# q and k projections of all units ahead of attention, as 2x2 block products with seven products for eight

## The chip, the cores and the metric

The kernel runs on one core of a Trainium2 chip. The metric is the device time of one execution in microseconds (us). Engines are called PE (TensorE, matmuls and transposes), DVE (VectorE), ACT (ScalarE), POOL (GpSimd) and SP (SyncE, which issues most DMAs). Each engine runs its own instructions in their order; semaphores make one wait for another.

## What is computed

One layer of a transformer block on x of 1024 x 1024 in float32. The part that the change touches:

```python
h = rms_norm(x, g_pre_mix[l])
proj = h @ w_in[l]
sb_q, sb_k, sb_v = jnp.split(proj[..., :c0], 3, axis=-1)      # 8 heads of 64
d_q, d_k, d_v = jnp.split(proj[..., c0:c1], 3, axis=-1)        # 4 heads of 2 x 64
gates = jax.nn.sigmoid(proj[..., c1:])                          # 2 x 1024 columns
y_sb = stick_breaking_attention(sb_q, sb_k, sb_v)               # sigmoids and a running product
y_diff = differential_attention(q1, q2, k1, k2, d_v, lam, bias) # two softmaxes, one subtracted
merged = gate_sb * (y_sb @ w_sb_out[l]) + gate_diff * (y_diff @ w_diff_out[l])
x = x + rms_norm(merged @ w_o[l], g_post_mix[l])
```

An MLP with a squared ReLU follows (1024 to 4096 and back).

## The kernel before

Float32 accuracy comes from splitting: each operand is kept as a rounded part "hi" and a rest "lo", and a product is three matmuls, hi by hi, hi by lo, lo by hi. `load_split` (L95) loads a block of weights of 128 x 1024 (0.5 MB) on SP, casts it on ACT (L102) and subtracts on DVE (L103). h stands transposed in SBUF as h_hi and h_lo for the whole attention stage; `normalised` (L155) and `transpose_h` (L174) make it in two halves c of 512 rows.

Attention has eight units of work: four stick-breaking ones with two heads each (`steps_sb`, `finish_sb`), then four differential ones with one head, which is two maps (`steps_diff`, `finish_diff`). Per head or map there are eight query tiles of 128 rows, taken in pairs j in the order 3, 1, 2, 0. A pair's step issues its scores z (L262, L263), sigmoids on ACT (L322, L323), a mask on POOL (L326), a scan and a product on DVE (L331, L332); a step later its finish transposes the weights on PE (L281), splits them (ACT L287, DVE L288) and multiplies by v (L300, L301). In differential units DVE adds the bias and takes the minimum (L389), ACT takes the exponential, DVE combines both maps (L403, L404).

The queries and keys of a unit are made inside the unit before it. `prepare(u + 1)` (L463) yields pieces of `project_q`, `project_k` (16 blocks in all, each 2 x 24 matmuls of 512 columns in `project`, L189) and, every second unit, `project_v` for two units (8 tiles of 24 matmuls of 256 columns). Their accumulators acc_sbq, acc_sbk, acc_sbv, acc_dfq, ... are split into half tiles by ACT and DVE (L210, L211, L225, L226), and k is copied to the other half of the partitions by four DMAs (L230, L231). The gates (16 blocks like those of q, with their results kept in DRAM) are filler too: eight go into attention by the table GATES (L35), eight follow it (L530). The loop at L511 mixes a step, the finish of the step before, and pieces of filler by the steps' weights. A scheduler then sets the final order of the instructions on each engine, from dependences, buffers and the order written.

Pools limit what can be early: two accumulators "acc" for filler, two each of "sc", "av" and "tr" in PSUM; four tiles each of qs, kh and kl, three of v (each unit has one), four of w for split weights, two of raw.

Behind attention come the product with w_mix (L567), w_o (L656), the up projection, which takes 2x2 blocks with seven products already (L778 and the sums at L732 to L735 on POOL), and the down projection (L954).

## Time and profile before

| | |
|---|---|
| median of 3 runs | 1458.88 us (1458.36 to 1459.6) |
| span of the profiled execution | 1456.6 us |
| first scores to first product with w_mix | about 34 to 648 us |
| DMA, mean over the span | 151 GB/s |
| granted clock of PE, mean | 0.999 |

The profile holds one execution; its own time is its span and about 2 us around it, by the runs. "Busy" is the time in which an engine had an instruction in hand. The page cuts the span into 40 slices of 36 us and gives each engine's busy share in tenths (9 is 90% or more), and what the DMAs moved:

```profile
PE   7999999999999999999999999999999999999997
DVE  5477988898779876635556499767665669754783
POOL 2022322231000000000002335333330357232611
GB/s 206 73 138 64 72 48 81 65 73 48 83 85 66 75 122 180 162 196 139 162 120 244 238 151 195 187 151 142 143 161 205 252 286 178 209 243 273 197 287 58
```

PE is busy in all slices but the first and the last. DVE's share is highest in slices 4 to 10, the stick-breaking units.

### The profile page before, as it was taken

The numbers are of one execution on the slowest core, as the hardware profiler recorded it, in microseconds if no ns is written. First come the engines' busy times: TensorE is split into PE (matmuls) and PEld (weight loads), VectorE is DVE, ScalarE is ACT, GpSimd is POOL, SyncE is SP. The second block draws the span as 40 slices with busy tenths as digits, with TensorE's granted clock in tenths as the row PEclk, the third lists the DMA queues.
The fourth block names the chain that finished last, engine by engine and source line by source line (L and its number), as shares of the span: only waits on it lengthen the run. The fifth ranks groups of instructions, "written<-read, shape, count | busy, mean of one in ns | idle before, by whom it ended". The sixth has DMA issues, their size and how long they took to land.

```text
span 1456.6 us, 20071 instructions
## 1 busy us (share of the span) xinstructions
PE 1435.0 (99%) x7302; PEld 1220.3 (84%) x7302; DVE 1016.5 (70%) x1468; ACT 742.3 (51%) x1352; POOL 321.2 (22%) x312
## 2 busy tenths in 40 slices
PE   7999999999999999999999999999999999999997
PEld 6888898899889888888888878888888888888886
DVE  5477988898779876635556499767665669754783
ACT  6355765676556554763335364444444443534350
POOL 2022322231000000000002335333330357232611
PEclk9999999999999999999999999999999999999999
DMA  5241212221322245553437745544446785677681
GB/s 206 73 138 64 72 48 81 65 73 48 83 85 66 75 122 180 162 196 139 162 120 244 238 151 195 187 151 142 143 161 205 252 286 178 209 243 273 197 287 58
DMA packets 93946, 220.50 MB, mean 151 GB/s; under 512 B 9260, under 2 KB 24856, under 8 KB 93848
## 3 DMA queue, kind: packets, MB, share of 16 engines
q1 hardware_dynamic: 79448, 199.30, 42.8%
q10 hardware_dynamic: 14400, 19.93, 3.8%
q8 instruction: 57, 0.93, 0.3%
q14 instruction: 41, 0.34, 0.1%
HBM read 153.11 MB, written 60.05 MB: 146 GB/s over the span
## 4 chain that ended last, share of the span: by engine, by line
PE 94%; DVE 2%; DMA 1%; issue 1%; ACT 1%; POOL 0%; SPq 0%; POOLq 0%; DVEq 0%; ACTq 0%
PE dS L954 12%; PE dA L954 9%; PE mix L567 6%; PE o L656 6%; PE p_tr L778 5%; PE p_av L778 5%; PE c L778 4%; PE acc_gate L198 4%; PE acc_gate L196 4%; PE acc_gate L197 4%; PE p_sc L778 3%; PE z L263 2%; PE z L262 2%; PE tr_sb L281 2%; PE p L778 1%
## 5 line engine op out<-in xcount | busy, mean ns | idle before, releaser
L331 DVE TENSOR_TENSOR_SCAN rest<-rest 128x896 f32<-128x896 f32 (+3 forms) x64 | 87.6, 1374 | 20.6 <-POOL rest L326 20.3
L198 PE MATMUL acc_gate<-h_hi,lo_gate 128*128 128x512 f32 x256 | 101.0, 394 | 0.0
L196 PE MATMUL acc_gate<-h_hi,hi_gate 128*128 128x512 f32 x256 | 100.8, 394 | 0.0
L197 PE MATMUL acc_gate<-h_lo,hi_gate 128*128 128x512 f32 x256 | 100.7, 394 | 0.0
L608 DVE TENSOR_TENSOR lS_lo<-raw_S,lS_hi 128x1024 fp32r<-128x1024 f32 x32 | 56.2, 1757 | 39.8 <-ACT lS_hi L607 39.8
L326 POOL TENSOR_SCALAR_AFFINE_SELECT rest<-rest 128x128 f32<-128x128 f32 x64 | 23.5, 367 | 240.7 <-ACT rest L322 232.1
L954 PE MATMUL dS<-rT_hi,lS_hi 128*128 128x512 f32 x192 | 74.7, 389 | 0.0
L954 PE MATMUL dS<-rT_lo,lS_hi 128*128 128x512 f32 x192 | 74.7, 389 | 0.0
L954 PE MATMUL dS<-rT_hi,lS_lo 128*128 128x512 f32 x192 | 74.7, 389 | 0.0
L607 ACT CAST lS_hi<-raw_S 128x1024 fp32r<-128x1024 f32 x32 | 33.7, 1052 | 74.1 <-DMA raw_S<-s_dramS 33.8
L567 PE MATMUL mix<-y,hi_mix 128*128 128x512 f32 x256 | 68.6, 389 | 0.0
L394 ACT ACTIVATE s<-s,low 128x896 f32<-128x896 f32 (+7 forms) x64 | 49.7, 777 | 29.9 <-DVE low L389 29.7
L389 DVE CUSTOM_DVE_ANT_0 s<-z,bias 128x512 f32<-128x512 f32 (+3 forms) x64 | 37.0, 587 | 32.4 <-PE z L263 26.4
L567 PEld LDWEIGHTS mix<-y,hi_mix 128*128 128x128 f32 x256 | 48.0, 188 | 10.0
L198 PEld LDWEIGHTS acc_gate<-h_hi,lo_gate 128*128 128x128 f32 x256 | 48.2, 188 | 9.2
L197 PEld LDWEIGHTS acc_gate<-h_lo,hi_gate 128*128 128x128 f32 x256 | 48.2, 188 | 8.8
L196 PEld LDWEIGHTS acc_gate<-h_hi,hi_gate 128*128 128x128 f32 x256 | 48.2, 188 | 8.6
L116 POOL TENSOR_SCALAR rstd_o<-s 128x1 f32<-128x1 f32 x8 | 2.8, 356 | 236.5 <-DVE wa_lo L608 212.2
L287 ACT CAST wth_sb<-tr_sb 128x512 fp32r<-128x512 f32 (+1 forms) x80 | 41.2, 548 | 26.6 <-PE tr_sb L281 25.2
L326 POOL TENSOR_SCALAR_AFFINE_SELECT beta<-beta 128x128 f32<-128x128 f32 x64 | 53.9, 842 | 3.4 <-ACT beta L323 2.4
L288 DVE TENSOR_TENSOR wtl_sb<-tr_sb,wth_sb 128x512 fp32r<-128x512 f32 (+1 forms) x80 | 48.5, 627 | 7.7 <-ACT wth_sb L287 7.5
L778 PE MATMUL c<-hB_hi,wa_hi 128*128 128x512 f32 x128 | 50.0, 392 | 2.1 <-ACT p L798 2.1
(351 smaller groups left out, 4751.2 us busy)
## 6 DMA issues: line engine op xcount, KB each, us to landing
s_dramS<-us SPq DMA_DIRECT2D x64, 256.0 KB, 3.9
raw_S<-s_dramS SPq DMA_DIRECT2D x32, 512.0 KB, 4.4
s_dramA<-u ACTq DMA_DIRECT2D x48, 256.0 KB, 3.5
raw_A<-s_dramA SPq DMA_DIRECT2D x24, 512.0 KB, 3.8
raw_gate<-in_w_in_dram SPq DMA_DIRECT2D x16, 512.0 KB, 3.7
gate_dram<-gt SPq DMA_DIRECT2D x32, 256.0 KB, 2.5
y<-y_dram SPq DMA_DIRECT2D x16, 512.0 KB, 6.4
g<-gate_dram SPq DMA_DIRECT2D x16, 512.0 KB, 4.3
```

What stands on the lines that cost most here:

```text
L196: nc.tensor.matmul(acc, w_hi[:, ks], h_hi[k][:, cs], start=(k == 0), stop=False)
L197: nc.tensor.matmul(acc, w_hi[:, ks], h_lo[k][:, cs], start=False, stop=False)
L198: nc.tensor.matmul(acc, w_lo[:, ks], h_hi[k][:, cs], start=False, stop=(k == NK - 1))
L288: nc.vector.tensor_tensor(lo[:, :n], tr[:, :n], f32(hi[:, :n]), op=ALU.subtract)
L326: nc.gpsimd.affine_select(tl[:, dg], tl[:, dg], pattern=[[-1, P]], compare_op=ALU.is_gt, fill=fill, base=0, channel_multiplier=1,)
L331: nc.vector.tensor_tensor_scan(back, back, back, 1.0, op0=ALU.mult, op1=ALU.bypass)
L394: e = nc.scalar.activation(s[:, :nk], s[:, :nk], AF.Exp, bias=low, scale=-1.0, accum_out=sums[:, m:m + 1],)
L567: nc.tensor.matmul(accs[i][c], st[:, ks], mv[:, cs], start=(first and k % 4 == 0), stop=(last and k % 4 == 3),)
L608: nc.vector.tensor_tensor(lo, raw, f32(hi), op=ALU.subtract)
L656: nc.tensor.matmul(accs[n], st, mv[:, n * HALF:(n + 1) * HALF], start=(first and k == 0), stop=(last and k == NK - 1),)
L778: nc.tensor.matmul(acc, st[:, ks], mv, start=(first and k == 0 and i == 0), stop=(k == 3 and i == 2), skip_group_check=True,)
L954: nc.tensor.matmul(acc, st[:, e, ts], mv[:, e, :], start=(first and e == 0 and i == 0), stop=(last and e == 1 and i == 2))
```

## The change

A stage of its own now makes all q and k, with buffers of its own (23 "leaf" tiles of 0.5 MB, 8 "half" tiles of 0.25 MB). The two weight blocks of a unit (q and k) are the rows of a 2x2 block matrix, each cut into two halves of 512 along the model dimension; h is cut into four blocks, by model half and by row half. A Strassen-like scheme (in Winograd's form) needs seven block products of 12 matmuls (128 x 512, over 4 blocks of 128, three each) where the plain one has eight.

`first_two` computes the two products with h blocks 11 and 21, whose sum is q of the first rows; product one is also kept in DRAM. The sums T1 to T4 of h blocks are made once, on DVE and POOL, and split. `pair_sums` makes four sums of weights on POOL for each unit, `last_five` splits them, issues five products into the banks sc, av and tr, and adds them on DVE. `put` splits each quarter of the result and stores it to qk_dram on ACT's queue. The second row half of h is split again at the end (`split_late`), one part of it after a trip through DRAM.

In attention `load_qk(u + 1)` loads the ready parts at the start of unit u by 12 DMAs of 0.25 MB on SP. Filler is v (in odd units) and gates alone; 14 gates are now in attention, 2 behind it. The steps and finishes, the filler's loads and its evictions are issued with high priority for the scheduler.

```diff
-GATES = [range(0, 2), range(2, 2), range(2, 4), range(4, 4), range(4, 6), range(6, 6), range(6, 8), range(8, 8)]
+GATES = [range(0, 3), range(3, 4), range(4, 7), range(7, 8), range(8, 10), range(10, 11), range(11, 13), range(13, 14)]
...
+        def product_h(acc, w, name, first=True, last=True):
+            w_hi, w_lo = w
+            for k in range(4):
+                ks = slice(k * P, (k + 1) * P)
+                b_hi, b_lo = right_block(name, k)
+                for i, (st, mv) in enumerate(((w_hi, b_hi), (w_hi, b_lo), (w_lo, b_hi))):
+                    nc.tensor.matmul(
+                        acc, st[:, ks], mv, start=(first and k == 0 and i == 0), stop=(k == 3 and i == 2),
+                        skip_group_check=True,
...
+        def put(n, which, c, src):
+
+            stage = leaf(f"qk_{n}_{which}_{c}")
+            hi, lo = stage[:, 0, :], stage[:, 1, :]
+            if which == 0:
+                scale = SCALE if n < N_SB else -SCALE
+                nc.scalar.activation(hi, src, AF.Copy, scale=scale)
+                nc.vector.scalar_tensor_tensor(lo, src, scale, f32(hi), op0=ALU.mult, op1=ALU.subtract)
+            else:
+                nc.scalar.copy(hi, src)
+                nc.vector.tensor_tensor(lo, src, f32(hi), op=ALU.subtract)
+            nc.scalar.dma_start(out=qk_dram[n][:, which, :, c * HALF:(c + 1) * HALF], in_=f32(stage))
...
+        def first_two(n0, ws):
+
+            accs = [acc_tile(f"p12_{n0 + e}") for e in range(2)]
+            for e in range(2):
+                product_h(accs[e], halves(ws[e], 0), "B11")
+                p1 = half(f"p1_{n0 + e}")
+                nc.scalar.copy(p1, accs[e])
+                nc.sync.dma_start(out=p1_dram[n0 + e], in_=p1)
+            for e in range(2):
+                product_h(accs[e], halves(ws[e], 1), "B21", first=False)
+                put(n0 + e, 0, 0, accs[e])
...
+            for f, blk in zip((f0, f1), blks):
+                nc.sync.dma_start(out=f, in_=w_in[blk])
+            s1 = half(f"s1_{n}")
+            a11, a12, a21, a22 = (f[:, i * HALF:(i + 1) * HALF] for f in (f0, f1) for i in range(2))
+            nc.gpsimd.tensor_tensor(s1, a21, a22, op=ALU.add)
+            nc.gpsimd.tensor_tensor(a21, a11, a21, op=ALU.subtract)
+            nc.gpsimd.tensor_tensor(a11, s1, a11, op=ALU.subtract)
+            nc.gpsimd.tensor_tensor(a12, a12, a11, op=ALU.subtract)
+            return n, {"T1": s1, "T2": a11, "B22": a12, "T3": a21, "T4": a22}
...
+        def split_one(n, raw):
+            ring[0] += 1
+            if ring[0] % 2:
+                w = stream.tile([P, 2, HALF], F32R, tag="w", name=f"ws_{ring[0]}", bufs=4)
+            else:
+                w = big_pair(f"wl_{ring[0]}")
+            hi, lo = w[:, 0, :], w[:, 1, :]
+            nc.scalar.copy(hi, raw)
+            nc.vector.tensor_tensor(lo, raw, f32(hi), op=ALU.subtract)
+            return hi, lo
...
+        def last_five(n, ws):
+            b, d, c = (ps.tile([P, HALF], F32, tag=t, name=f"p_{t}{n}", bufs=2) for t in ("sc", "av", "tr"))
+            v, q, u21 = half(f"v_{n}"), half(f"q_{n}"), half(f"u21_{n}")
+            nc.sync.dma_start(out=v, in_=p1_dram[n])
+            w = {name: split_one(n, ws[name]) for name in ("T2", "T3", "T1", "T4", "B22")}
+            product_h(b, w["T2"], "T2")
+            nc.vector.tensor_tensor(v, b, v, op=ALU.add)
+            product_h(d, w["T3"], "T3")
+            nc.vector.tensor_tensor(q, d, v, op=ALU.add)
+            product_h(c, w["T1"], "T1")
+            nc.vector.tensor_tensor(q, c, q, op=ALU.add)
+            put(n, 1, 1, q)
+            product_h(d, w["T4"], "T4", first=False)
+            nc.vector.tensor_tensor(u21, d, v, op=ALU.add)
+            put(n, 1, 0, u21)
+            product_h(c, w["B22"], "B22", first=False)
+            nc.vector.tensor_tensor(v, c, v, op=ALU.add)
+            put(n, 0, 1, v)
...
+        first_two(0, ws)
+        normalise(1, xs1)
+        transpose_h(1, xs1)
+        for j in range(2):
+            whole_again(j)
+        first_two(2, [load_split(w_in[blocks_of(n)[0]], f"wa{n}") for n in (2, 3)])
+        r11, r21, r12, r22 = (raws[j, c] for j, c in ((0, 0), (1, 0), (0, 1), (1, 1)))
+        for q in range(2):
+            nc.sync.dma_start(out=r12_dram[q], in_=r12[q])
+        sums_h["T2"] = [leaf(f"t2_{q}", None, F32) for q in range(2)]
+        sums_h["T1"], sums_h["T3"], sums_h["T4"] = r11, r12, r21
+        for q in range(2):
+            nc.vector.tensor_tensor(r11[q], r12[q], r11[q], op=ALU.subtract)
+            nc.vector.tensor_tensor(sums_h["T2"][q], r22[q], r11[q], op=ALU.subtract)
+        for q in range(2):
+            nc.gpsimd.tensor_tensor(r12[q], r22[q], r12[q], op=ALU.subtract)
+        for q in range(2):
+            nc.gpsimd.tensor_tensor(r21[q], r21[q], sums_h["T2"][q], op=ALU.subtract)
+        first_two(4, [load_split(w_in[blocks_of(n)[0]], f"wa{n}") for n in (4, 5)])
+        split_sum("T2")
+        split_sum("T3")
+        first_two(6, [load_split(w_in[blocks_of(n)[0]], f"wa{n}") for n in (6, 7)])
+        summed = pair_sums(0)
+        split_sum("T1")
+        split_sum("T4")
+        split_late(1, r22)
+        for n in range(n_units):
+            ready = summed[1]
+            if n + 1 < n_units:
+                summed = pair_sums(n + 1)
+            last_five(n, ready)
+        r12 = [leaf(f"r12_again{q}", None, F32) for q in range(2)]
+        for q in range(2):
+            nc.sync.dma_start(out=r12[q], in_=r12_dram[q])
+        split_late(0, r12)
...
+        def load_qk(u):
+
+            qs, kh, kl = ([pa.tile([P, S], F32R, tag=n, name=f"{n}_{u}_{a}", bufs=4) for a in range(2)] for n in ("qs", "kh", "kl"))
+            for a, own in enumerate((LO, HI)):
+                for part in (LO, HI):
+                    nc.sync.dma_start(out=f32(qs[a][part]), in_=qk_dram[u][own, 0, 0 if part is LO else 1, :])
+                    nc.sync.dma_start(out=f32(kh[a][part]), in_=qk_dram[u][own, 1, 0, :])
+                    nc.sync.dma_start(out=f32(kl[a][part]), in_=qk_dram[u][own, 1, 1, :])
+            return qs, kh, kl
...
         def fill(u, gates):
-            if u + 1 < n_units:
-                yield from prepare(u + 1)
+            if u + 1 < n_units and u % 2:
+                yield from values(u + 1)
             for b in gates:
                 yield from gate(b)
...
+            if u + 1 < n_units:
+                operands[u + 1] = load_qk(u + 1)
+            size = 2 * len(GATES[u]) + (4 if u % 2 and u + 1 < n_units else 0)
             total = 36 * (2 if u < N_SB else 1)
-            for weight, finish in (steps_sb(u, *operands[u]) if u < N_SB else steps_diff(u - N_SB, *operands[u])):
-                if waiting is not None:
-                    waiting()
+            steps = steps_sb(u, *operands[u], vs[u]) if u < N_SB else steps_diff(u - N_SB, *operands[u], vs[u])
+            while True:
+                with tc.high_priority(offset=1500):
+                    weight, finish = next(steps, (0, None))
+                    if finish is not None and waiting is not None:
+                        waiting()
+                if finish is None:
+                    break
```

How instructions move, at three places. First PE at the end of unit 0 (names: tr_sb, z, av with unit, head, then pair or query tile; acc_sbq2 is filler for unit 2). In the kernel before, the first scores of unit 1 stand among filler:

```order
L262 MATMUL z_1_0_6_0_1576<-kh_sbk1_0_955,qs_sbq1_0_804 128x512
L263 MATMUL z_1_0_6_0_1576<-kl_sbk1_0_957,qs_sbq1_0_804 128x512
L262 MATMUL z_1_0_6_512_1581<-kh_sbk1_0_955,qs_sbq1_0_804 128x384
L263 MATMUL z_1_0_6_512_1581<-kl_sbk1_0_957,qs_sbq1_0_804 128x384
L198 MATMUL acc_sbq2_1_1667<-h_hi3_158,lo_sbq2_1635 128x512
L196 MATMUL acc_sbq2_1_1667<-h_hi4_159,hi_sbq2_1634 128x512
L197 MATMUL acc_sbq2_1_1667<-h_lo4_167,hi_sbq2_1634 128x512
L198 MATMUL acc_sbq2_1_1667<-h_hi4_159,lo_sbq2_1635 128x512
L196 MATMUL acc_sbq2_1_1667<-h_hi5_160,hi_sbq2_1634 128x512
L197 MATMUL acc_sbq2_1_1667<-h_lo5_168,hi_sbq2_1634 128x512
L198 MATMUL acc_sbq2_1_1667<-h_hi5_160,lo_sbq2_1635 128x512
L196 MATMUL acc_sbq2_1_1667<-h_hi6_161,hi_sbq2_1634 128x512
```

In the changed kernel the same attention work stands closely together:

```order
L460 MATMUL tr_sb0_1_2_1_2611<-ident_69,beta_0_1_4_2474 128x128
L460 MATMUL tr_sb0_1_2_1_2611<-ident_69,beta_0_1_5_2492 128x128
L460 MATMUL tr_sb0_1_2_1_2611<-ident_69,beta_0_1_4_2474 128x128
L460 MATMUL tr_sb0_1_2_1_2611<-ident_69,beta_0_1_5_2492 128x128
L441 MATMUL z_1_0_7_0_2681<-kh_1_0_1897,qs_1_0_1895 128x512
L442 MATMUL z_1_0_7_0_2681<-kl_1_0_1899,qs_1_0_1895 128x512
L479 MATMUL av_0_1_2_2597<-wth_sb0_1_2_0_2603,v_v0_0_1634 128x256
L441 MATMUL z_1_0_7_512_2686<-kh_1_0_1897,qs_1_0_1895 128x512
L442 MATMUL z_1_0_7_512_2686<-kl_1_0_1899,qs_1_0_1895 128x512
L480 MATMUL av_0_1_2_2597<-wtl_sb0_1_2_0_2604,v_v0_0_1634 128x256
L479 MATMUL av_0_1_2_2597<-wth_sb0_1_2_0_2603,v_v0_0_1634 128x256
L480 MATMUL av_0_1_2_2597<-wtl_sb0_1_2_0_2604,v_v0_0_1634 128x256
```

The filler of this place is gone: what PE had between a split on DVE and the matmul that reads it is now other attention work. The next filler rows are acc_v1_2, 37 rows further on.

Second, DVE at the same place. Before, with evictions of q and k (L211, L226) and a split of weights (L103) between the scans (L331, printed as SCALAR_TENSOR_TENSOR) and the products (L332):

```order
L103 TENSOR_TENSOR lo_sbv2_0_2053<-raw_sbv2_0_2050,hi_sbv2_0_2052 128x1024
L211 SCALAR_TENSOR_TENSOR qs_sbq2_0_1630<-acc_sbq2_1_1667,qs_sbq2_0_1630 64x512
L288 TENSOR_TENSOR wtl_sb0_1_2_2_1560<-tr_sb0_1_2_2_1555,wth_sb0_1_2_2_1559 128x384
L211 SCALAR_TENSOR_TENSOR qs_sbq2_1_1631<-acc_sbq2_1_1667,qs_sbq2_1_1631 64x512
L331 SCALAR_TENSOR_TENSOR rest_1_0_7_1593<-rest_1_0_7_1593 128x1024
L288 TENSOR_TENSOR wtl_sb0_1_0_0_1616<-tr_sb0_1_0_0_1611,wth_sb0_1_0_0_1615 128x384
L332 TENSOR_TENSOR beta_1_0_7_1592<-beta_1_0_7_1592,rest_1_0_7_1593 128x1023
L226 TENSOR_TENSOR kl_sbk2_0_1783<-acc_sbk2_0_1791,kh_sbk2_0_1781 64x512
L304 TENSOR_TENSOR part_0_1_2_1567<-av_0_1_2_1528,part_0_1_2_1567 64x256
L331 SCALAR_TENSOR_TENSOR rest_1_0_2_1697<-rest_1_0_2_1697 128x384
```

In the changed kernel (L510 is the scan, L511 the product, L467 the split of transposes, L483 and L486 the finish):

```order
L467 TENSOR_TENSOR wtl_sb0_1_2_1_2617<-tr_sb0_1_2_1_2611,wth_sb0_1_2_1_2616 128x512
L511 TENSOR_TENSOR beta_1_0_6_2661<-beta_1_0_6_2661,rest_1_0_6_2662 128x895
L510 SCALAR_TENSOR_TENSOR rest_1_0_7_2680<-rest_1_0_7_2680 128x1024
L467 TENSOR_TENSOR wtl_sb0_1_2_2_2629<-tr_sb0_1_2_2_2624,wth_sb0_1_2_2_2628 128x384
L486 TENSOR_TENSOR yt_0_1_1_2539<-part_0_1_1_2536,yt_0_1_1_2539 64x256
L467 TENSOR_TENSOR wtl_sb0_1_0_0_2703<-tr_sb0_1_0_0_2698,wth_sb0_1_0_0_2702 128x384
L511 TENSOR_TENSOR beta_1_0_7_2679<-beta_1_0_7_2679,rest_1_0_7_2680 128x1023
L510 SCALAR_TENSOR_TENSOR rest_1_0_2_2848<-rest_1_0_2_2848 128x384
L510 SCALAR_TENSOR_TENSOR rest_1_0_3_2861<-rest_1_0_3_2861 128x512
L483 TENSOR_TENSOR part_0_1_2_2636<-av_0_1_2_2597,part_0_1_2_2636 64x256
```

The evictions of q and k are gone from here, and attention's own instructions follow each other.

Third, SP where the new stage goes from first_two to last_five (raw_wa is the first weight block of a unit for first_two, fw the two blocks of a unit for pair_sums, v the re-read of product one). All of it is new:

```order
L98 DMA raw_wa6_624<-in_w_in_dram 128x1024
L98 DMA raw_wa7_630<-in_w_in_dram 128x1024
L280 DMA p1_dram4_164<-p1_4_558 128x512
L293 DMA fw0_0_700<-in_w_in_dram 128x1024
L280 DMA p1_dram5_165<-p1_5_573 128x512
L280 DMA p1_dram6_166<-p1_6_650 128x512
L293 DMA fw0_1_701<-in_w_in_dram 128x1024
L318 DMA v_0_745<-p1_dram0_160 128x512
L280 DMA p1_dram7_167<-p1_7_665 128x512
L293 DMA fw2_0_841<-in_w_in_dram 128x1024
```

fw0_1 stands behind raw_wa7, whose buffer it takes once that is split, and behind p1_dram6, a store of a product.

219 lines of the change are left out of this document (117 added, 102 removed).

## The prediction

> **What bounds the kernel now.** I read the page's busy times first, then the chain that ended last, then what TensorE (PE) waits for, then the table of stages.
>
> ```profile
> span 1456.6 us, 20071 instructions
> PE 1435.0 (99%) x7302; PEld 1220.3 (84%) x7302; DVE 1016.5 (70%) x1468; ACT 742.3 (51%) x1352; POOL 321.2 (22%) x312
> PE 94%; DVE 2%; DMA 1%; issue 1%; ACT 1%; POOL 0%; SPq 0%; POOLq 0%; DVEq 0%; ACTq 0%
> ...
> PE trx L178 <- DVE x L170: 7.7, 2, 7.5
> PE c L778 <- ACT p L798: 2.1, 1, 2.1
> PE p_sc L778 <- ACT w_hi L607: 1.2, 1, 1.2
> ```
>
> PE is busy 1435.0 of 1456.6 us. The rest is 21.6 us, 7.7 of it the wait for the first rows of x and only 3.3 in the two waits behind attention. So a matmul taken away is worth its full price only while nothing new waits, and work that PE does beside another engine's work is cover. The stages show how thick that cover is (each row: the stretch, its length, then busy us of PE, weight loads, DVE, ACT, POOL; clock, DMA share, GB/s):
>
> ```profile
> 0.00:33.00 33.00, 24.01 (x133) 20.06 (x134) 17.89 (x24) 21.12 (x34) 8.09 (x24) 1.00 0.65 228
> 172.00:294.00 122.00, 122.00 (x759) 109.37 (x758) 102.97 (x153) 77.43 (x181) 31.33 (x53) 1.00 0.23 66
> 368.00:654.00 286.00, 286.00 (x1591) 248.88 (x1590) 198.09 (x510) 167.38 (x352) 0.43 (x3) 1.00 0.39 122
> 860.00:1145.00 285.00, 284.40 (x1252) 234.96 (x1253) 205.66 (x224) 142.59 (x213) 84.16 (x56) 1.00 0.52 172
> ```
>
> In stick-breaking attention (172 to 294 is the second unit and what surrounds it) PE has no gap, but VectorE (DVE) is busy 103 of 122 us, 84%. The change takes PE work out of just this stage. The last row is the up projection, which already runs a seven-product scheme: PE 284.4 of 285. That speaks for the new projection stage.
>
> **What goes.** Prices of matmuls are start to start, since a duration of 0.39 us holds latency that overlaps. The first and last of 32 rows with 512 columns, and of 17 with 256:
>
> ```profile
> 1145.01 0.39 PE L954 MATMUL dA<-rB_lo,lA_hi 128*128 128x512 f32 x1
> 1152.04 0.39 PE L954 MATMUL dA<-rB_hi,lA_lo 128*128 128x512 f32 x1
> ...
> 23.72 0.28 PE L244 MATMUL acc_sbv<-kl_sbv,h_hi 128*128 128x256 f32 x1
> 25.64 0.28 PE L245 MATMUL acc_sbv<-qs_sbv,h_lo 128*128 128x256 f32 x1
> 40.01 1.91 PE L178 MATMUL trx<-ident,x 128*128 128x128 f32 x16
> ```
>
> 7.03 / 31 = 0.227 us for 512 columns, 1.92 / 16 = 0.12 for 256, 1.91 / 16 = 0.12 for a transpose. q and k took 16 blocks x 48 = 768 matmuls; the change takes 8 units x 7 products x 12 = 672. 96 x 0.227 = **-21.8 us**, the whole gain.
>
> **What attention has left.** Its DVE work, in groups over the four stick-breaking units, then the four differential ones (a count, then busy us and mean ns):
>
> ```profile
> L331 DVE TENSOR_TENSOR_SCAN rest<-rest 128x896 f32<-128x896 f32 (+3 forms) x64 | 87.6, 1374 | 20.6 <-POOL rest L326 20.3
> L288 DVE TENSOR_TENSOR wtl_sb<-tr_sb,wth_sb 128x512 fp32r<-128x512 f32 (+1 forms) x80 | 48.5, 627 | 7.7 <-ACT wth_sb L287 7.5
> L332 DVE TENSOR_TENSOR beta<-beta,rest 128x895 f32<-128x895 f32 (+3 forms) x64 | 47.9, 753 | 2.0
> L307 DVE TENSOR_TENSOR yt<-part,yt 64x256 fp32r<-64x256 f32 x32 | 13.2, 414 | 0.5 <-ACT yt L306 0.5
> ...
> L389 DVE CUSTOM_DVE_ANT_0 s<-z,bias 128x512 f32<-128x512 f32 (+3 forms) x64 | 37.0, 587 | 32.4 <-PE z L263 26.4 <-DMA bias<-bias_rows 5.7
> L404 DVE SCALAR_TENSOR_TENSOR s<-s,sums,s 128x896 f32<-128x896 f32 (+7 forms) x32 | 26.0, 812 | 0.4
> L288 DVE TENSOR_TENSOR wtl_df<-tr_df,wth_df 128x512 fp32r<-128x512 f32 (+1 forms) x40 | 24.4, 629 | 7.2 <-ACT wth_df L287 7.2
> L389 DVE CUSTOM_DVE_ANT_0 s<-z,bias,low 128x384 f32<-128x384 f32 (+3 forms) x32 | 17.5, 546 | 5.9 <-PE z L263 4.8
> L403 DVE TENSOR_SCALAR s<-s,sums 128x896 f32<-128x896 f32 (+7 forms) x32 | 16.6, 517 | 0.7
> L364 DVE SCALAR_TENSOR_TENSOR y<-y,subln,w 128x256 f32<-128x256 f32 x16 | 7.7, 480 | 0.3
> ...
> L103 DVE TENSOR_TENSOR lo_gate<-raw_gate,hi_gate 128x1024 fp32r<-128x1024 f32 x16 | 19.5, 1221 | 8.8 <-ACT hi_gate L102 6.8 <-PE avd L344 2.0
> L255 DVE TENSOR_TENSOR v_sbv<-acc_sbv,v_sbv 128x128 fp32r<-128x128 f32 x32 | 8.8, 281 | 8.2 <-ACT v_sbv L254 8.1
> L211 DVE SCALAR_TENSOR_TENSOR qs_sbq<-acc_sbq,qs_sbq 64x512 fp32r<-64x512 f32 x16 | 11.0, 689 | 7.7 <-ACT qs_sbq L210 7.3
> ```
>
> Stick-breaking units: 87.6 + 48.5 + 47.9 + 2 x 13.2 (L304 is as long as L307) = 210 us. v costs 16 x 0.28 + 2 x 1.22 = 6.9, a gate 1.22, q and k of one unit 8 x 0.69 + 2 x 1.22 = 7.9. On PE a head's 4608 score columns run twice (4.1 us), with 36 transposes (4.3), 32 value matmuls of 256 columns (3.8) and 8 of 128 (0.5): 25.4 us a unit, 101 in all; a v is 192 x 0.12 = 23.0, a gate 48 x 0.227 = 10.9, q and k of a unit 21.8. Before, these units carry four pairs of q and k, two v and four gates: PE 101 + 87 + 46 + 44 = 278, DVE 210 + 32 + 14 + 5 = 261, or 94%, and PE never waited. After, two v and eight gates: PE 101 + 46 + 87 = **234**, DVE 210 + 14 + 10 = **234**. The cover of 17 us is gone.
>
> Differential units: 37.0 + 17.5 + 26.0 + 24.4 + 16.6 = 121.5, and seven ops like L364 in each of 16 finishes, here 6.7 to 7.7 us a group, some 48; with read-outs of low and small ops about 188 us. After, one v and eight gates (two behind the last unit): DVE 188 + 7 + 10 = 205; PE 4 x 20.5 (as above with four short matmuls more per finish) + 23 + 87 = 192. Rows overlap a little at their ends (172 to 294 is 84% where the sums make 94%, part of it other work), so DVE is between 180 and 205 there.
>
> Where both engines need the same time, PE's idle time is set by how filler is spread. The order shows two places that I can price. At the end of unit 0 PE has 88 matmuls and transposes in a row, worth 11.2 us, of which only seven are filler: the v tiles have three buffers, so the evictions of the first two v1 products wait for unit 0's v, and both accumulators are held. In that stretch DVE has 23 instructions: two scans of 896 and 1024 (2.02 + 2.29), two mults (1.09 + 1.22), four shorter scans, seven splits of transposes, and small ones, 15.5 us with its two v splits. PE idles 15.5 - 11.2 = 4.3 us. v2 in unit 3 meets the same limit at the end of unit 2: about 5. In the differential units fill is drawn forward: between the first scores of units 5 and 6 PE has about 37 us of work and DVE 47 to 51, so 10 to 14 us, of which the transfer of the surplus before it gives back some; I take 11. Together **+20 us**; bounds 5 (DVE's slack of 6% as before is enough, only the two ends of units count half) and 40 (12.8 of DVE surplus, 9 at the two places, and every other unit's start and end at 3).
>
> **The projection stage.** Its PE work is 0.227 x 672 = 153 us. Prices from like rows of the up projection:
>
> ```profile
> L732 POOL TENSOR_TENSOR s<-raw_up 128x512 f32<-128x512 f32 x8 | 13.3, 1662 | 98.3 <-DMA raw_up<-in_w_up_dram 91.6 <-DVE w_lo L608 6.7
> L607 ACT CAST w<-s 128x512 fp32r<-128x512 f32 x16 | 9.9, 621 | 28.7 <-PE p_av L778 27.5 <-DVE hT_lo L608 0.7 <-POOL up L733 0.5
> L608 DVE TENSOR_TENSOR w<-s,w 128x512 fp32r<-128x512 f32 x16 | 21.7, 1359 | 0.1
> L865 DVE TENSOR_TENSOR v<-p_sc,p 128x512 f32<-128x512 f32 x12 | 8.2, 684 | 0.3 <-PE p_sc L778 0.3
> raw_gate<-in_w_in_dram SPq DMA_DIRECT2D x16, 512.0 KB, 3.7
> L608 DVE TENSOR_TENSOR rT_lo<-t,rT_hi 128x1024 fp32r<-128x1024 f32 x16 | 36.0, 2250 | 8.5 <-ACT rT_hi L607 8.5
> L608 DVE TENSOR_TENSOR rT_lo<-b_d,rT_hi 128x1024 fp32r<-128x1024 f32 x8 | 9.7, 1218 | 0.2 <-ACT rT_hi L607 0.2
> ```
>
> A unit's last five products are 60 x 0.227 = 13.6 us of PE. Beside them DVE has 5 PSUM adds and 3 put splits at 0.68 and 5 operand splits at 0.68 to 1.36: 8.8 to 12.3; ScalarE (ACT) 8 x 0.62 = 5; GpSimd (POOL) 4 x 1.66 = 6.6; SP two loads and one read. All hide: 0, up to 5 if the joints don't. The switch into this part hardly hides: fw0_1 stands on SP behind the store of p12_6's first product, when PE has some 45 products left (10.2 us); then 3.7 of load, three POOL ops (s1_1 lies between) of 1.66, one cast 0.62 and a split of 0.68 to 1.36 come to 10.0 to 10.7 us, and each of six hand-overs costs something more: +2 (0 to 5). At the start pair 0/1 has only 48 matmuls on the first half of x, where now the v products fill in; x_7 is the tenth load of 0.5 MB, 5.2 MB at 228 GB/s = 23 us, then its square, scale and turn: +3 (1 to 4). Later wa loads: +1 (0 to 2). The stage together **+6** (1 to 16). Its put DMAs stand on ACT's queue, ACT has half its time free.
>
> **The turn into attention.** SP's twelve loads of unit 0 (3.1 MB, some 14 us at 228 GB/s) stand behind the re-read of r12 and wait until the stored q and k have landed; behind them wait tables and later loads. v0's 23 us cover them. Then first scores, sigmoids, select, scan and mult (near 8 us) stand before the first transpose, with some 5 us of gate to fill: **+3** (0 to 5). Later loads start a unit ahead: 0. The L230 copies and 64 evictions go, but PE never waited for them: 0.
>
> **Sum.** 1456.6 - 21.8 + 20 + 6 + 3 = 1463.8 us of span. The median of the runs, 1458.88, is 2.3 above the profiled span, so **1466** us.
>
> **A rule against it.** The rows above show the same 128x1024 subtraction at 2250 ns where POOL has just written and goes on, and at 1218 where it isn't. The Trainium skill, "SBUF — State Buffer", section "SBUF: two separate sides", says that DVE with two SBUF inputs and POOL exclude each other for whole instructions. By that rule the projection's splits and h sums pay POOL's time as well; the 1359 ns row agrees. As a mechanism of this kernel: 5 splits at 0.68 + 1.66 instead of at most 1.36 add 4.9 to DVE's 12.3, 17.2 a unit against PE's 13.6, so 8 x 3.6 = 29 us. That gives 1495.
>
> **Rivals.** *PE stays the bound.* For it: 284.4 of 285 in the up projection, and the sums' overlap; then attention costs 5 to 12, the stage 1 to 5, the turn 0 to 2: 1443 to 1456, faster. *DVE decides in attention* at 40: 1486. It decides from the point at which a unit has under 58 us of PE work for 58 of DVE, and single joints don't average out. *POOL and DVE exclude each other*, above: 1495. *The clock.* The wait of 2.1 us at 854 left the clock at 1.00; the transposes after the opening 7.5 us took 3.06 us for 12, 0.25 each instead of 0.12:
>
> ```profile
> 7.48 3.06 PE L178 MATMUL trx<-ident,x 128*128 128x128 f32 x12 [7.48 <-DVE x L170]
> ```
>
> If three or four new gaps grow to 5 us and each is followed by 3 us at half pace, that adds 1.5 each: 1472. The Trainium skill, "TensorE: Matmul & The Clock Gate", section "HAM oscillation", puts the limit at about 3.4 us of idle time; no run here shows where it lies.
>
> **How the numbers follow.** Forecast (1462 to 1476) 0.34; PE stays the bound 0.33; the middle of the two, within 0.2%, about what a measurement of this kernel can tell from no change, 0.13; DVE decides (1476 to 1492) 0.13; POOL and DVE 0.05; clock 0.02. Faster 0.33, same 0.13, slower 0.54. The range takes in both ends of attention's term: 1443 to 1490.
>
> **What would show it.** PE busy near 1413 shows the gain. PE's waits should name DVE splits and scans in attention, above all around the ends of units 0 and 2 and between units 5 and 6, in sum 15 to 25 us, and DVE's busy share there should be above 90%. A wait of 1 to 4 us on the first of the last five products, and last-five units at 13.6 us each, would confirm the stage. Wrong: idle time under 10 us in attention (then faster), or a unit's last five at 16 us and more.

## The result and the profile after

The changed kernel takes 1533.66 us (median of 4 runs, 1531.92 to 1534.44) against 1459.24 of the kernel before on the same chip: a ratio of **1.0505**, 95% interval 1.0489 to 1.0521. It is slower, as forecast, but by 74 us and not by 7.

The page of the changed kernel (span, busy time of each engine, granted clock in 40 slices, shares of the chain that ended last):

```profile
span 1531.6 us, 20277 instructions
PE 1453.2 (95%) x7206; PEld 1217.3 (79%) x7206; DVE 1071.4 (70%) x1520; ACT 742.5 (48%) x1362; POOL 405.0 (26%) x356
PEclk9899989999999999998999999999999999999999
PE 74%; DVE 9%; DMA 7%; issue 4%; ACT 3%; POOL 2%; SPq 1%; ACTq 0%; DVEq 0%; POOLq 0%
```

The 96 matmuls are gone (7302 to 7206), yet PE is busy 18 us longer: the clock row falls below 9 in three slices, and at half clock matmuls of 512 columns start 0.43 us apart (864 to 866 us) instead of 0.227. PE's share of the chain fell from 94% to 74%; DVE, DMA and ACT took its place.

What PE waited for, costliest first (total us, times, longest):

```profile
PE av L480 <- DVE wtl_sb L467: 9.1, 8, 1.7
PE z L441 <- DVE low L568: 8.7, 10, 4.0
PE mix L722 <- DMA y<-y_dram: 8.1, 2, 6.6
PE trx L202 <- DVE x L186: 7.8, 2, 7.4
PE ss L534 <- ACT sqp L531: 6.0, 1, 6.0
PE bp L612 <- DMA oh<-in_onehot_dram: 3.5, 1, 3.5
PE p L247 <- DVE qk L262: 3.1, 1, 3.1
```

Of these only the fourth stood in the list before (as 7.7 us). The list sums to much less than the 75 us that the span grew, so I used a second measure. **Lost time** of a stretch is its length less its matmuls at their undisturbed prices (0.227 us for 512 columns and 0.12 for 256, as in the prediction; 0.17 for 384, 0.06 for 128, 0.11 for a transpose). It holds idle time, half clock and starts that stand too far apart. Each number is summed over all PE rows of one profiled execution:

| stretch (marked by PE's matmuls) | lost before | lost after | more | forecast |
|---|---|---|---|---|
| start to first v product (projection stage) | 12.3 | 28.6 | +16.3 | +6 |
| first v to first scores to last scores (turn, attention) | 15.7 | 66.4 | +50.7 | +3, +20 |
| last scores to end of w_mix (drain) | 0.5 | 24.0 | +23.5 | 0 |
| w_o, up, down (to the last matmul) | 5.0 | 11.4 | +6.4 | 0 |
| matmul work itself | | | -21.7 | -21.8 |
| sum | | | +75.2 | +7.2 |

The spans differ by 75.0. Of the 50.7 in the second row, 17.0 lie in the 70 us from 200 to 270, the turn, and 33.7 further on (the 15.7 of before are all taken off the second). In the kernel before, the first scores start at 65.0 us, not at about 34, and those of units 1 and 2 at 142 and 206.

Units do not stand at the same time in all kernels. So here is lost time by unit, from the first scores of one to those of the next (each unit has 24 matmuls z of L441; in whole us, by the same prices, good to about 1 us), with three kernels of the experiments below:

| kernel | unit 0 with the turn | units 1 to 3 | units 4 to 7 |
|---|---|---|---|
| before | 2 | 6 | 5 |
| changed | 15 | 23 | 25 |
| gates where they were | 20 | 40 | 26 |
| four units ahead | 19 | 11 | 9 |
| no product behind the scan | 13 | 6 | 26 |

Windows of the changed kernel, by 20 us, then the whole of unit 5, then two spells of half clock (each row: the stretch, its length, busy us of PE, weight loads, DVE, ACT, POOL; clock, DMA share, GB/s):

```profile
280.00:300.00 20.00, 17.13 (x124) 15.33 (x124) 19.30 (x28) 15.59 (x38) 13.08 (x13) 1.00 0.59 138
400.00:420.00 20.00, 17.22 (x126) 15.28 (x125) 18.11 (x29) 13.64 (x36) 7.47 (x13) 1.00 0.35 89
420.00:440.00 20.00, 13.87 (x99) 11.89 (x98) 19.46 (x31) 13.17 (x34) 8.98 (x11) 1.00 0.30 64
520.00:540.00 20.00, 14.05 (x104) 12.50 (x104) 13.66 (x46) 9.70 (x28) 0.14 (x1) 0.98 0.57 145
720.00:740.00 20.00, 11.80 (x37) 8.97 (x38) 4.61 (x11) 4.64 (x8) 0.00 (x0) 0.76 0.23 79
...
529.10:579.40 50.30, 42.25 (x299) 37.70 (x298) 43.15 (x137) 30.46 (x83) 0.14 (x1) 0.97 0.39 102
...
218.00:231.00 13.00, 12.89 (x28) 6.78 (x29) 10.99 (x13) 4.64 (x11) 7.57 (x8) 0.51 1.03 226
720.00:726.00 6.00, 5.01 (x12) 4.03 (x13) 0.90 (x3) 2.12 (x4) 0.00 (x0) 0.50 0.14 46
```

Three different pictures. In stick-breaking units (first three rows) DVE is busy 97% in two of the windows and 91% in the third, while PE has holes. From 520 to 540 and from 720 to 740 no engine is full: that is a chain with nothing beside it. And after a gap the clock halves while PE is fully "busy" (the row from 218). Over the execution, (1 - clock) x busy share of PE in windows of 1 us sums to 23 us, in nine spells; in the kernel before it is 0.0 (its clock is recorded from 12 us on).

The drain before, at its own place in the program, had eight gates beside the last unit's chain:

```profile
620.00:640.00 20.00, 20.00 (x99) 16.81 (x98) 7.91 (x16) 14.41 (x24) 0.00 (x0) 1.00 0.65 226
640.00:660.00 20.00, 20.00 (x91) 16.56 (x89) 6.76 (x12) 8.22 (x12) 0.00 (x0) 1.00 0.52 185
```

The places of the largest gaps, from the timeline of the changed kernel (start, duration, engine, instruction, in brackets the idle time before it and what ended that; a row with no bracket followed at once):

```profile
38.16 0.69 DVE L222 CAST h<-r 128x1024 fp32r<-128x1024 f32 x1
38.88 3.48 DVE L223 TENSOR_TENSOR h<-r,h 128x1024 fp32r<-128x1024 f32 x1
42.29 1.21 DVE L355 TENSOR_TENSOR r<-r,r 128x1024 f32<-128x1024 f32 x1
43.43 1.21 DVE L103 TENSOR_TENSOR lo_wa<-raw_wa,hi_wa 128x1024 fp32r<-128x1024 f32 x1
44.56 0.68 DVE L262 SCALAR_TENSOR_TENSOR qk<-p,qk 128x512 fp32r<-128x512 f32 x1
...
45.30 1.22 PE L247 MATMUL p<-h,hi_wa 128*128 128x512 f32 x2 [3.12 <-DVE qk L262]
...
217.96 1.17 PE L612 MATMUL bp<-oh,tbl 32*4 32x384 f32 x2 [3.50 <-DMA oh<-in_onehot_dram]
...
538.49 0.69 DVE L568 CUSTOM_DVE_ANT_0 s<-z,bias 128x512 f32<-128x512 f32 x1 [4.35 <-DMA bias<-bias_rows]
539.25 0.79 PE L441 MATMUL z<-kh,qs 128*128 128x512 f32 x1 [4.02 <-DVE low L568]
...
720.99 0.58 PE L534 MATMUL ss<-sqp,ones 128*128 128x256 f32 x1 [6.02 <-ACT sqp L531]
739.16 2.93 PE L722 MATMUL mix<-y,hi_mix 128*128 128x512 f32 x6 [6.64 <-DMA y<-y_dram]
```

In the projection stage the accumulator's eviction (L262) stands on DVE behind `split_late`, two h sums and a weight split. At 218 the matmuls of the bias table, in order on PE, wait for a small table that SP loads among the 12 q and k loads. At 538 a bias row's load (L551) stands on SP among the q and k loads of the next unit. At 721 and 739 PE waits for the last unit's normalisation, its store and its re-read.

### The profile page after: what moved, and what is told of

Same layout as the page of the kernel before. It is cut to its first block, busy times and chain, and to the rows that moved or that the text cites. A ratio compares the mean times of both kernels' runs of the same rounds, so it can differ in the third digit from the quotient of the medians.

```text
span 1531.6 us, 20277 instructions
## 1 busy us (share of the span) xinstructions
PE 1453.2 (95%) x7206; PEld 1217.3 (79%) x7206; DVE 1071.4 (70%) x1520; ACT 742.5 (48%) x1362; POOL 405.0 (26%) x356
## 4 chain that ended last, share of the span: by engine, by line
PE 74%; DVE 9%; DMA 7%; issue 4%; ACT 3%; POOL 2%; SPq 1%; ACTq 0%; DVEq 0%; POOLq 0%
PE dS L1109 11%; PE dA L1109 9%; PE mix L722 5%; PE c L933 4%; PE p_av L933 4%; PE p_tr L933 4%; PE acc_gate L393 3%; PE acc_gate L391 3%; PE acc_gate L392 3%; PE p_av L247 3%; PE o L811 3%; PE p_tr L247 2%; PE p_sc L933 2%; PE z L441 2%; PE p L247 2%
## 5 line engine op out<-in xcount | busy, mean ns | idle before, releaser
L510 DVE TENSOR_TENSOR_SCAN rest<-rest 128x896 f32<-128x896 f32 (+3 forms) x64 | 87.8, 1374 | 30.8 <-POOL rest L505 30.6
L391 PE MATMUL acc_gate<-h,hi_gate 128*128 128x512 f32 x256 | 102.3, 400 | 0.6 <-ACT gt L636 0.6
L393 PE MATMUL acc_gate<-h,lo_gate 128*128 128x512 f32 x256 | 102.0, 398 | 0.7 <-DVE lo_gate L103 0.7
L392 PE MATMUL acc_gate<-h,hi_gate 128*128 128x512 f32 x256 | 101.8, 398 | 0.0
L722 PE MATMUL mix<-y,hi_mix 128*128 128x512 f32 x256 | 75.7, 411 | 8.8 <-DMA y<-y_dram 8.1
L441 PE MATMUL z<-kh,qs 128*128 128x512 f32 (+2 forms) x192 | 72.5, 379 | 11.4 <-DVE low L568 8.7
L423 PE MATMUL acc_v<-hi_v,h 128*128 128x256 f32 x256 | 72.9, 286 | 0.0
L421 PE MATMUL acc_v<-hi_v,h 128*128 128x256 f32 x256 | 72.2, 285 | 0.0
L422 PE MATMUL acc_v<-lo_v,h 128*128 128x256 f32 x256 | 72.1, 283 | 0.0
L501 ACT ACTIVATE rest<-z 128x512 f32<-128x512 f32 (+2 forms) x96 | 46.0, 495 | 48.8 <-PE z L442 36.0
L762 ACT CAST lS_hi<-raw_S 128x1024 fp32r<-128x1024 f32 x32 | 33.7, 1052 | 74.0 <-DMA raw_S<-s_dramS 42.0
L442 PE MATMUL z<-kl,qs 128*128 128x512 f32 (+2 forms) x192 | 67.7, 355 | 0.0
L505 POOL TENSOR_SCALAR_AFFINE_SELECT beta<-beta 128x128 f32<-128x128 f32 x64 | 61.2, 957 | 22.1 <-ACT beta L502 21.0
L391 PEld LDWEIGHTS acc_gate<-h,hi_gate 128*128 128x128 f32 x256 | 48.8, 191 | 11.6 <-DVE rest L510 1.3
```

The source lines that it names most:

```text
L391: nc.tensor.matmul(acc, w_hi[:, ks], b_hi, start=(k == 0), stop=False)
L392: nc.tensor.matmul(acc, w_hi[:, ks], b_lo, start=False, stop=False)
L393: nc.tensor.matmul(acc, w_lo[:, ks], b_hi, start=False, stop=(k == NK - 1))
L421: nc.tensor.matmul(acc[:, :256], a_hi, w_hi[:, ks], start=(k == 0), stop=False)
L423: nc.tensor.matmul(acc[:, :256], a_lo, w_hi[:, ks], start=False, stop=(k == NK - 1))
L441: nc.tensor.matmul(z[:, :c1 - c0], q, kh[:, c0:c1], start=True, stop=False)
```

## The experiments

Each kernel is the changed one with the edit named there (the two that load unit 1 later also ask for the tables first), and each is timed beside the kernel before (1461.0, 1462.2, 1461.3 and 1462.4 us in the four groups). Two runs of one kernel differed by up to 13 us, so a difference of a few us in time is not read; lost time comes from one profile each.

**Gates where they were.** Six of the gates go back behind attention.

```diff
-GATES = [range(0, 3), range(3, 4), range(4, 7), range(7, 8), range(8, 10), range(10, 11), range(11, 13), range(13, 14)]
+GATES = [range(0, 2), range(2, 2), range(2, 4), range(4, 4), range(4, 6), range(6, 6), range(6, 8), range(8, 8)]
```

> Gates spread as in the kernel before: 2,0,2,0,2,0,2,0 in the units, eight behind the last one. Theory (attention has too little filler, and the drain behind unit 7 has none): the 33 us lost between the last scores and the end of the product with w_mix fall to under 10, but attention loses 65 us of filler where DVE is as long as PE, so its loss of about 41 us grows to 65 to 80: 1530 to 1550 us in all. Rival (only the gates are in the wrong place): the drain's loss goes and attention's stays near 41: about 1508.

1530.67 us (ratio 1.048, 1.037 to 1.059). The drain's loss is gone, 24.0 to 0.8; turn and attention lose 89.7 for 66.4. Its windows over the drain:

```profile
700.00:720.00 20.00, 20.00 (x97) 16.74 (x96) 7.45 (x16) 15.38 (x23) 0.00 (x0) 1.00 0.52 193
720.00:740.00 20.00, 20.00 (x91) 16.56 (x90) 6.75 (x13) 7.47 (x11) 0.00 (x0) 1.00 0.40 132
```

PE is full, as before the change. So the gates that the change moved forward are what the drain lacks. But units 1 to 3 now lose 40 for 23, and the sum over both stages stays at 90: moving the gates back only moves the hole.

**Four units ahead.** Units 0 to 3 keep the new stage; units 4 to 7 get q and k with eight products inside attention, as before, and three gates more stand behind it.

```diff
-GATES = [range(0, 3), range(3, 4), range(4, 7), range(7, 8), range(8, 10), range(10, 11), range(11, 13), range(13, 14)]
+GATES = [range(0, 3), range(3, 4), range(4, 7), range(7, 7), range(7, 8), range(8, 8), range(8, 9), range(9, 11)]
-        first_two(4, [load_split(w_in[blocks_of(n)[0]], f"wa{n}") for n in (4, 5)])
-        first_two(6, [load_split(w_in[blocks_of(n)[0]], f"wa{n}") for n in (6, 7)])
-        for n in range(n_units):
+        for n in range(4):
...
+            if 4 <= u + 1 < n_units:
+                yield from prepare(u + 1)
```

> Only units 0 to 3 have q and k made ahead with seven products; those of units 4 to 7 are filler in units 3 to 6 with eight, as in the kernel before; gates 3,1,3,0,1,0,1,2 and five behind unit 7. PE work is 10.9 us more than in the change. Theory (attention and its drain need some 270 us of filler and the change has 244; here there are 331): the loss between first scores and the end of w_mix falls from 88 to 25 to 40 us, 1485 to 1505 in all. Rival (the order by priority or the stage ahead is what costs, not the amount of filler): over 1515.

1519.59 us (ratio 1.040, 1.036 to 1.045), the least of all. That misses the theory's 1485 to 1505 and lies where the rival was put, over 1515. Attention and drain lose 44.3 for 88.4, a little more than the 25 to 40 of the theory, and the priorities are the same, so it is filler that they lacked. But the projection stage loses 43.9 for 28.6, which the theory did not count. Its windows at the switch and around the first scores of unit 3 (at 359.2 here, at 417.6 in the changed kernel, so these rows stand for its rows from 400 to 440):

```profile
40.00:60.00 20.00, 2.85 (x10) 1.59 (x8) 20.00 (x10) 9.57 (x11) 17.56 (x8) 0.64 0.20 76
...
340.00:360.00 20.00, 19.91 (x115) 17.15 (x113) 15.42 (x20) 13.10 (x29) 4.16 (x10) 1.00 0.18 54
360.00:380.00 20.00, 19.58 (x111) 17.01 (x112) 17.11 (x25) 13.04 (x29) 2.04 (x8) 1.00 0.24 61
```

At this end of unit 2 PE is busy 39.5 of 40 us where the changed kernel had 31.1, and DVE's work is spread over a longer unit. At the switch, with half of the `first_two` products, PE stands nearly empty while DVE works through all 20 us and POOL through 17.6 on splits and sums: this work of the seven-product scheme is paid once, whatever the number of units, and needs cover too.

**More filler.** Nine gates are computed twice (432 matmuls, 98 us; the text below counts eight).

```diff
+GATES = [[0, 1, 2, 0], [3, 3], [4, 5, 6, 4], [7, 7], [8, 9, 8], [10], [11, 12, 11], [13]]
+        for b in (14, 15, 14, 15, 14):
```

> Eight gates are computed twice (the result is the same), five of them in the units, three behind unit 7: 384 matmuls, 87 us, more for PE as filler, and 10 us more for DVE. Theory (PE's time from the first scores to the end of w_mix is lost for lack of filler): the 88 us lost there fall to 45 to 60, so the time rises by 45 to 60 only, to 1580 to 1595. Rival (PE is lost in chains and joints that filler does not reach): the time rises by 80 or more, to 1614 or above.

1599.82 us, 66 more for 98 us of work. Attention and drain lose 53.4 for 88.4: a third of the added work went into holes, as the theory said.

**No product behind the scan.** The multiplication by the running product on DVE is left out (L511, 47.9 us of DVE in the prediction's group).

```diff
-                        nc.vector.tensor_tensor(
-                            beta[:, :nk - 1], beta[:, :nk - 1], rest[:, 1:nk], op=ALU.mult
-                        )
```

> Leaves out part of the computation: the product of beta and the scanned rest (L511, 64 DVE instructions, 48 us), so the weights are beta alone. PE's work stays as it is. Theory (DVE is as long as PE in the stick-breaking units, so its time is PE's lost time): 15 to 30 us less than 1533.7, all of it between the first scores and about 500 us; the loss at 400 to 440 (13 us) falls under 5. Rival (PE's losses there are chains of latency or late loads, whatever DVE's rate): under 8 us less.

1519.72 us (ratio 1.040), 13.9 less, just under the least that the theory expected. Attention loses 45.9 for 64.4. The 40 us around the first scores of unit 3 (here at 401.9, so 16 us earlier than in the changed kernel) read:

```profile
384.00:404.00 20.00, 20.00 (x130) 18.03 (x130) 13.04 (x19) 14.10 (x34) 4.87 (x12) 1.00 0.39 113
404.00:424.00 20.00, 18.76 (x147) 17.52 (x146) 17.71 (x27) 15.04 (x39) 7.13 (x12) 1.00 0.43 99
```

DVE is down from 37.6 to 30.8 of 40, PE up from 31.1 to 38.8; the loss goes from 13 to 3 us. Units 1 to 3, whose product is gone, lose 6 for 23, units 4 to 7, which have none, 26 for 25, and the drain 4 more. So DVE's work decides in the stick-breaking units. Whether it is DVE's rate or the chain of a head stays open: the edit also takes one step out of the chain of scan, product and transpose.

**Eight products ahead.** The stage computes plain products, without sums of h and weights.

```diff
+        def plain(n, which, c, w):
+            acc = any_tile(f"pl_{n}_{which}_{c}")
+            product_h(acc, halves(w, 0), f"B1{c + 1}")
+            product_h(acc, halves(w, 1), f"B2{c + 1}", first=False)
+            put(n, which, c, acc)
...
+        for n in range(1, n_units):
+            ws = both(n)
+            for which in range(2):
+                for c in range(2):
+                    plain(n, which, c, ws[which])
```

> The stage stays ahead of attention, but with the plain eight products a unit: 96 matmuls more, no sums of h and of weights, no trip of h through DRAM. Theory (the loss lies behind the stage; the scheme of seven is nearly as cheap as planned): the 21.8 us come back, less the 10 us that the stage loses at its joints: 1540 to 1550. Rival (the scheme's sums, splits and transfers are what costs): under 1525.

1549.46 us (ratio 1.061), inside the theory's range, but by other terms. The stage loses 12.9, no more than the 12.3 of before, so a stage of its own is not what costs there: the sums and splits of the scheme are, 15.7 us of the 21.8 that it saves. Attention (69.3 for 64.4) and drain (27.9 for 24.0) lose no less than with seven products: that loss comes with the products made ahead and the change's gates and priorities, not with the scheme.

**Evictions earlier on DVE.** Two edits aim at the gap at 42 us. In the first, `put` gets a higher priority and the two buffers of fw change places.

```diff
-            stage = leaf(f"qk_{n}_{which}_{c}")
+            with tc.high_priority(offset=600):
+                stage = leaf(f"qk_{n}_{which}_{c}")
-            if n % 2:
+            if n % 2 == 0:
```

> Two joints inside the projection stage: unit 0's weights for the sums take the free fw buffers instead of the raw ones that are still in use (odd units change with even ones), and the stores of results have priority over the sums of h on DVE. Theory (3.1 and 2.1 us of wait there, each followed by half clock, 10.7 us lost between 44 and 79): 6 to 10 us less than 1533.7. Rival (POOL's and DVE's rate in the stage sets the pace): 0 to 3 us less, the wait moves a few us on.

1527.8 us, but the stage's loss is 30.0 for 28.6 and the gap at 42 is 3.57 us long for 3.12, so the 6 us of time don't come from there and the theory fails. The second puts `split_late(1)` on DVE behind the evictions of unit 7.

```diff
-        split_late(1, r22)
+        split_late(1, r22, put_split[7, 0])
```

> The late split of unit 7's second quarter and its sums stand on VectorE behind the splits of the first quarter's q and k, so that the projections of units 2 and 3 are split about 7 us earlier. Theory (the stage's loss at 40 to 60 us is VectorE's order): the gap of 3.1 us at 42 us and the half clock from 44 to 51 us are gone and the loss of the projection stage falls from 28.6 by 5 to 7 us. Rival (VectorE's and GpSimd's load at the switch sets the pace, and a wait moves to the seven products that are then late): the stage's loss falls by 0 to 3 us.

1541.94 us (ratio 1.055), the stage's loss 31.1. The gap at 42 and the half clock after it are gone, as the theory said, and a longer one opens later. In the timeline (POOL's weight sums, the cast on ACT that waits for them, the product that waits for the cast):

```profile
72.57 4.46 POOL L306 TENSOR_TENSOR fw<-s,fw 128x512 f32<-128x512 f32 x2
74.84 0.62 ACT L319 CAST ws<-fw 128x512 fp32r<-128x512 f32 x1 [2.47 <-POOL fw L306]
75.51 0.80 PE L255 MATMUL p_sc<-hT_hi,ws 128*128 128x512 f32 x1 [5.99 <-ACT ws L319]
```

The rival holds: the load of DVE and POOL at the switch sets the pace, and order only says where the wait shows.

**Sums on DVE.** The sums and differences of h that POOL makes go to DVE.

```diff
-            nc.gpsimd.tensor_tensor(r12[q], r22[q], r12[q], op=ALU.subtract)
+            nc.vector.tensor_tensor(r12[q], r22[q], r12[q], op=ALU.subtract)
...
-            nc.gpsimd.tensor_tensor(r21[q], r21[q], sums_h["T2"][q], op=ALU.subtract)
+            nc.vector.tensor_tensor(r21[q], r21[q], sums_h["T2"][q], op=ALU.subtract)
```

> The sums of h (8 adds of 128x512 and 4 subtractions of 128x1024) go from POOL to DVE; the sums of weights stay on POOL. DVE has some 10 us more to do in the first 70 us. Theory (DVE and POOL exclude each other there: a subtraction of 1.23 us took 3.48 beside a POOL subtraction, and the store's split behind it came too late for PE): the wait of 3.1 us at 42 and the 7 us at half clock go, 4 to 8 us less than 1533.7 between 40 and 80. Rival (DVE simply has too much to do there): 5 or more us longer in that stretch.

1536.46 us; the stage loses 26.6 for 28.6, too little for either side: 2 us less from 40 to 60 and 1 more from 60 to 80. The subtraction of 3.48 us takes 1.23 now, the gap at 42 is 2.58 us long for 3.12 and the half clock behind it is gone. But DVE, which now makes the sums itself, is busy without a break from 41 to 49, and a spell of half clock at 73 stays. So the two do slow each other, and ending that alone doesn't pay.

**The bias tables.** `setup_bias`, whose matmuls wait at 218, goes into the projection stage (behind the sums of h, with buffers of that stage); or, in another kernel, ahead of the loads of unit 0, which the diff shows.

```diff
+        setup_bias()
         operands[0] = load_qk(0)
         for _ in values(0):
             pass
-        setup_bias()
```

> The bias tables (three loads, three small matmuls, their stores) are made in the projection stage instead of behind the loads of q and k. Theory (one late transfer stops PE for 3.5 us, and PE then runs 13.5 us at half clock, 6.7 us more): 8 to 11 us less than 1533.7, the turn into attention at clock 1.00. Rival (attention's first steps wait for their own loads and scans there anyway): 0 to 3 us less, PE idle or at half clock in the same stretch for another reason.

1538.15 us. In the turn the theory holds, the clock stays at 1.00 until 251 and the first 70 us lose 11 for 17. But in the stage PE now stops for 3.57, 6.90 and 3.66 us, 17 us of half clock follow, and the stage loses 37.7 for 28.6.

> One line moved: the bias tables are asked for ahead of unit 0's q and k, not behind them. Theory (the three small matmuls on the tables stop PE for 3.5 us, as their loads stand behind twelve and more on SP, and the half clock that follows costs 6.7): 6 to 10 us less than 1533.7, with clock 1.00 from 200 to 240. Rival (q and k are then late by as much, and the first scores stop PE): 0 to 3 us less.

1536.34 us: the wait of 3.5 us is gone, and one of 5.33 at 244 takes its place, for gate accumulators whose eviction on ACT waits 9.0 us for an earlier gate's store. The gain is missing as the rival said, though by another wait than the one it named.

**Loads of unit 1 later.** With the tables first, `load_qk(u + 1)` is called at half of unit u; in the second kernel POOL also writes a column of unit 1's tiles behind its selects in unit 0, so that the 12 reads (3.1 MB) cannot start earlier.

```diff
+                if u + 1 < n_units and u + 1 not in operands and 2 * cost >= total:
+                    operands[u + 1] = load_qk(u + 1)
...
+                    mark = nc.gpsimd.memset(f32(tl[:, 0:1]), 0.0)
+                    after(mark, last_select[0])
```

> The bias tables are asked for ahead of unit 0's q and k, and the next unit's q and k at half of a unit instead of at its start. Theory (at the turn the DMA engines are full, 211 GB/s at a share of 1.0, so with the tables first a gate's store took 10 us and stopped ACT, then PE for 5.3 us): the loss between 200 and 270, 17 us in the change and 16 with the tables first, falls under 9, 6 to 10 us less than 1533.7. Rival (the first scans and splits of attention set it, transfers or not): loss of 14 or more there, 0 to 3 us less.

1540.19 us. The edit did not do what it should: SP still issued unit 1's reads from 220 to 240, and the accumulators waited 7.29 us. It says nothing on the theory.

> Small tables first, as before, and the 12 reads of unit 1's q and k (3.1 MB) held back by writes to their tiles until the middle of unit 0. Theory (the turn's loss of about 17 us is transfers: the read-backs of units 0 and 1 and the gate stores share full queues): the gate store takes about 3 us, PE's wait on the gate accumulators is under 1 us, the loss in 200 to 270 us is under 9 us, and the kernel is 6 to 10 us under the change's time (1523 to 1528). Rival (the turn is a chain of first scores, rows and gates with nothing ready for PE): the loss in 200 to 270 us stays at 14 us or more and the time within 4 us of 1534.

1531.65 us (ratio 1.048, 1.041 to 1.054). Two of its windows at the turn:

```profile
210.00:220.00 10.00, 9.57 (x61) 9.30 (x62) 4.45 (x9) 6.28 (x13) 2.40 (x2) 0.83 0.88 226
220.00:230.00 10.00, 9.26 (x46) 7.40 (x45) 9.63 (x11) 6.85 (x16) 5.90 (x9) 1.00 1.01 298
```

The loss from 200 to 270 is 8.0 for 17.0 and no accumulator waits over 0.8 us: half of the turn was the reads of unit 1 in front of what the first steps need (the tables first, alone, leave 15.7). But from 270 to 300 it loses 10.9 for 5.2, and the gate stores took 3.0 to 7.9 us, so the time is the same within its interval. The theory was right on the place and wrong on the gain.

**The drain's chain.** The last finish is issued with high priority.

```diff
-        waiting()
+        with tc.high_priority(offset=1500):
+            waiting()
```

> One line: the last finish gets the same priority as the others. Theory (in the drain, sigmoids of the gates and their table loads stand on ACT between the last finish's steps; ss waits 6.0 us for ACT): 5 to 10 us less than 1533.7, the loss from the last scores to the end of w_mix falls from 24 to 14 to 19. Rival (the drain is one long chain of dependent steps and nothing is there to fill it): 0 to 3 us less.

1532.01 us, the drain loses 23.0 for 24.0. This order doesn't shorten it; it is a chain with no filler beside it, as the rival said.

## Why the prediction was wrong

The direction and the gain were right, the size was not: 68 us are missing between forecast and time, 23.5 in the drain, 14 in the turn, 13.7 in attention, 10.3 in the projection stage and 6.4 behind. By the prediction's own terms:

- **What goes, -21.8.** Measured -21.7. But "PE busy near 1413" failed at 1453: 23 us of the 40 are half clock; the other 17 I put down to matmuls that start apart, within the latency that busy time covers, but did not count.
- **Attention, +20 (5 to 40).** Measured +33.7 without the turn, inside the bounds, and most of it at the three places that the text priced. At the end of unit 0 (280 to 320) 6.8 us are lost for 4.3, at the end of unit 2 (400 to 440) 12.8 for 5: there DVE is busy 93 and 94%, PE waits for DVE splits as named, and the run without the product shows that DVE's work decides. That is right in kind and too small in size.

  Between the first scores of units 5 and 6 (529.1 to 579.4) 13.4 are lost for 11. PE's work there is worth 36.9 us for the 37 forecast, but DVE is busy 43.2 of 50.3 us (86%), less than the 47 to 51 of the text, and 4.0 of the loss is a wait in which DVE itself waits for a bias row; so the near hit at this place is partly luck, and no run tests DVE in these units. The 5.0 of the last 13 us before the last scores had no price. What the new priorities cost or save was not tested alone. The text's row from 172 to 294, called the second unit, is mostly the third.
- **The drain, 0: the step that failed.** The text booked the gates as work of the units ("After, one v and eight gates (two behind the last unit)") and never asked what the eight gates behind the last unit had covered. They covered its chain of finish, normalisation, store and re-read. With two left it costs +23.5; with the gates put back, the drain loses 0.8. The same gates are then missing in the units, so the fault is wider than this place: the budget compared sums unit by unit and never asked how much filler attention and drain need together.
- **The turn, +3 (0 to 5).** Measured 17.0, 6.8 of it half clock. "v0's 23 us cover them" and "Later loads start a unit ahead: 0" were wrong: the reads of unit 1 follow those of unit 0 at once, DMA stands at 0.98 to 1.04 of its share from 200 to 230, and small tables queue among them. Holding these reads took 9 us off this place.
- **The projection stage, +6 (1 to 16).** Measured +16.3, just past the upper end. "All hide: 0, up to 5 if the joints don't" holds for the last five products: from 100 us to the first v it loses 0.7, the later units start every 13.6 us as forecast, and the wait on the first of these products, forecast at 1 to 4 us, is 2.1. The first 40 us lose 13.2, 12.3 of it there before. The loss lies from 40 to 100, at the switch, where sums and splits for all units come together; the run with eight products has none of it.
- **Later stages, not in the sum.** +6.4 in code that is the same; 7.8 to 15 among these kernels for 5.0 before. Most of it lies at two waits, 2.2 us at 860 (none before) and 3.0 at 928 (2.1 before), and the half clock behind each. Why these waits grew isn't settled.
- **The rivals.** "PE stays the bound" fell. "DVE decides in attention" is what happened in the stick-breaking units; that the whole comes to 34 of its 40 us is in part chance, as the differential units hold waits of another kind. "POOL and DVE exclude each other" put 3.6 us a unit on the last five products: some of their DVE splits did take up to 1.78 us for 0.68, but PE lost nothing by it. The clock got 0.02 and three or four gaps at 1.5 us each; it took 23 us in nine spells, in all of the stretches above, so it is not a cause of its own but a surcharge on gaps.

One number joins attention and drain. Moving q and k of units 1 to 7 ahead takes 7 x 21.8 = 153 us of filler out of both, and they lose 57 more, 0.37 us for each. Putting 87 us back (four units) won 44, 98 us of useless gates won 35: 0.5 and 0.36. The prediction asked in which unit the sum of PE's work falls below DVE's; the measured rate says that filler is worth a third to a half of its length, on average over these stages (the last two figures hold the turn, which hardly differs: 17, 20 and 19 us). No kernel here beats the one before; the best leaves half of the products in attention.
